# Mixer projections two column blocks at a time, with seven products for two or three of eight row pairs

## The chip, the cores and the metric

The kernel runs on one core of one Trainium2 chip. The metric is device time in microseconds (us) for the whole program: the median of three runs is 2322.91 us before the change (2322.89, 2323.82, 2322.91).

## The reference

A trunk of two layers over 256 tokens of width 2048, float32. Each layer is a token mixer beside a cross-attention to 256 memory tokens, one output projection, and a SwiGLU feed-forward net. Layer 0 has the HGRN2 mixer, layer 1 the GLA mixer. What matters here are the mixers' input projections:

```python
D_MODEL, SEQ = 2048, 256
MIX_WIDTH = 1536                      # the mixer's width
GLA_KEY_WIDTH = 768                   # GLA: 4 heads, key 192, value 384
def _hgrn2_mixer(hn, w_in, lb, onorm):
    proj = hn @ w_in                  # (256 x 2048) @ (2048 x 6656)
    q, f, i, g, xq = jnp.split(proj, [MIX_WIDTH, 2 * MIX_WIDTH, 3 * MIX_WIDTH, 4 * MIX_WIDTH], axis=-1)
    f = lb + (1.0 - lb) * jax.nn.sigmoid(f)
    ...
def _gla_mixer(hn, w_in, w_gk, b_gk, onorm):
    proj = hn @ w_in                  # q, k: 768 columns each; v, g: 1536 each
    ...
def reference(...):
    hn = _rmsnorm(h, norm_mix[layer])
    y, xq = _hgrn2_mixer(...) if layer % 2 == 0 else _gla_mixer(...)
    h = h + jnp.concatenate([y, xa], axis=-1) @ w_out[layer]
    gate, up = jnp.split(_rmsnorm(h, norm_ffn[layer]) @ w_gate_up[layer], 2, axis=-1)
    h = h + (jax.nn.silu(gate) * up) @ w_down[layer]
```

## The kernel before

**Tiles.** The 256 tokens are two tiles of 128, the 2048 rows of a weight matrix 16 blocks of 128, taken in eight row pairs. A weight tile comes from memory as float32 into `raw` (four buffers). `split` makes two tiles of it in TensorE's float32 format `F32R`: ScalarE casts it (L207, the high part), and VectorE subtracts that from the original (L208, the low part). Both lie in one of six `parts` buffers. Each product is three matmuls into one sum: high x high, high x low, low x high (L249 to L251). All sums live in eight PSUM banks. The left factors, transposed and split in the same way, are `Quad` tiles of four row blocks each (`hx` in layer 0, `hm` in layer 1; names end in `h` and `l`).

**Projections.** `project` takes one block of columns (512, or 384 for GLA's) through all 16 row blocks: per row pair 2 x 2 products, 12 matmuls for one block, and 24 for two blocks. The two sums are then read by ScalarE, which writes them to SBUF with the activation.

**The mixers.** `hgrn_group` runs three times, one group of four heads each: projections f, q, v, gate of 512 columns, one after the other. `gla_pair` runs twice, with two heads each: k and q of 384 columns, then gate and v of 384 columns for each of two heads. What lies between (the forget gates `F`, `K`, the decays `Th`, the masked scores `sl..` and `sd..`, reading the state, the gated norm, the transposes of the result) is cut into pieces, which `later` puts in a queue; `project` calls `step` after every second row block, and takes one piece each time.

**The feed-forward net.** `project_halves` already takes two column blocks at once, gate and up, and of its row pairs some ("S") with seven products in place of eight (24 matmuls become 21): a block has seven sums p1 to p7 in seven banks, and VectorE joins them at the block's end (L833). For that, an S pair takes differences of the four weight blocks on VectorE (L350 to L352) before they are split. Tiles are named by the pair's number: `parts185a` to `d`. The left factors come with forms for it (`s`, `u`, `z`, `d0` beside the four plain ones).

**What sets the order.** Each engine runs its instructions in the order of a list that a scheduler makes ahead of time, and so does the queue SP, which issues the DMAs. An instruction that waits holds up all that stand behind it on its engine.

Of the kernel before, what the change touches and what calls it, by code (L numbers as in the profile page):

```python
# [9 lines left out]
F32 = mybir.dt.float32  # L10
# [7 lines left out]
P = 128  # L18
# [17 lines left out]
def trunk_kernel(ctx: ExitStack, tc: tile.TileContext, x, mem, norm_mix, norm_ffn, norm_mem,  # L36
# [99 lines left out]
    class Quad:  # L136
# [5 lines left out]

        def put(self, k, n, ps, gain=None):
# [34 lines left out]
    def later(*pieces):  # L178
        pending.extend(pieces)
# [40 lines left out]
    def project(quads, order, w, c0, n, name, parts=None, prep=None, by_tile=None):  # L220
# [11 lines left out]
        for qis, ts in groups:  # L232
            for qi in qis:
# [5 lines left out]
                for k, (hi, lo) in enumerate(got[qi]):  # L239
# [4 lines left out]
                    for t in ts:  # L244
                        xh = quads[q].h[:, k, t * P:(t + 1) * P]
                        xl = quads[q].l[:, k, t * P:(t + 1) * P]
# [73 lines left out]

    def project_halves(forms, kinds, w, c0, c1, name):
# [15 lines left out]
        for p, kind in enumerate(kinds):  # L337
            i, raw = new_raw()

            for j, c in ((slice(0, 4, 3), c0), (slice(1, 3), c1)):  # L340
                nc.sync.dma_start(out=raw[:, j, :],
                                  in_=w[2 * p * P:(2 * p + 2) * P, c:c + 512].rearrange("(k p) c -> p k c", p=P))
            x = forms[p].get
            last = p == len(PAIRS) - 1
            if kind == "S":
                tt = nc.vector.tensor_tensor
                b00, = split(raw[:, 0:1, :], f"{i}a")
                b11, b10 = split(raw[:, 2:4, :], f"{i}b")

                tt(out=raw[:, 0:2, :], in0=raw[:, 0:4:2, :], in1=raw[:, 1:2, :].broadcast_to([P, 2, 512]), op=ALU.subtract)  # L350
                tt(out=raw[:, 2, :], in0=raw[:, 2, :], in1=raw[:, 0, :], op=ALU.add)  # L351
                tt(out=raw[:, 3, :], in0=raw[:, 3, :], in1=raw[:, 2, :], op=ALU.subtract)  # L352
                t5, t7 = split(raw[:, 0:2, :], f"{i}c")
                t6, t4 = split(raw[:, 2:4, :], f"{i}d")
                todo = {1: ("x00", b00), 2: ("x01", b10), 3: ("z", b11), 4: ("x11", t4), 5: ("s", t5), 6: ("u", t6),
                        7: ("d0", t7)}
# [19 lines left out]
    def h_quad(hq, q, gain, ss, name):  # L376

        for t in range(NT):
            square_sum(h[:, t, q * 512:(q + 1) * 512], ss[:, t, q:q + 1], f"{name}{q}{t}")

        def turn():
            hq[q] = make_quad(Quad("hq", f"{name}{q}"),
                              lambda k, t: h[:, t, (4 * q + k) * P:(4 * q + k + 1) * P],
                              lambda k: gain[:, 4 * q + k:4 * q + k + 1])

        later(turn)
# [48 lines left out]
    for l in range(2):  # L435
# [17 lines left out]
        if l == 0:  # L453
            load_params()
            hq, ss = {}, new_ss("ss_x")
            for q in range(NQ):
                h_quad(hq, q, g_mix[0], ss, "hx")
# [180 lines left out]
    def hgrn_group(w, g, hq, r, yq):  # L638
# [3 lines left out]
        def stage(c0, name, func):  # L642
            ps = project(hq, range(NQ), w, c0 + 512 * g, 512, f"h{name}{g}")
            tag, bufs = ("stg", 2) if name in "fq" else (name, 1)
            dst = work.tile([P, NT, 512], F32, tag=tag, name=f"{name}s{g}", bufs=bufs)
            for t in range(NT):
                nc.scalar.activation(out=dst[:, t, :], in_=ps[t], func=func, scale=r[:, t:t + 1])
            return dst
# [52 lines left out]
    def gla_pair(w, pr, dec, decay, hq, r, yq):  # L701
# [4 lines left out]
        def stage(c0, name):  # L706
            ps = project(hq, range(NQ), w, c0 + pr * 2 * DK, 2 * DK, f"g{name}{pr}")
# [41 lines left out]
        ks = stage(kw, "k")  # L749
        later(turn_k)  # L750
        qs = stage(0, "q")
# [206 lines left out]
```

## Time and profile before

| | |
|---|---|
| runs | 2322.89, 2323.82, 2322.91 us; median 2322.91 |
| profiled execution | 2322.1 us, of which the span is 2320.3 us |
| TensorE (PE) busy | 2297.6 us, 99% |
| VectorE (DVE) busy | 1887.7 us, 81% |
| ScalarE (ACT) busy | 1261.2 us, 54% |
| DMA | 435.51 MB, mean 188 GB/s |

A row of a timeline has the start in us from the span's start, the duration, the engine, the line of the program, and the operation with output, inputs and shape; in square brackets stands the idle time before it and what ended it. Instructions of an engine overlap in part: the next one starts before the last has ended, so that the cost of one in a row of them is the distance from start to start. A row of the table of stretches has the stretch, its length, the busy time of PE, of PE's weight loads, of DVE, of ACT and of POOL (each with the count of instructions), the granted TensorE clock, the share of DMA time and GB/s.

### The profile page before, as it was taken

To read this page: it belongs to the slowest core of one execution; us is meant where nothing else is said; L and a number is where in the kernel's file an instruction comes from. 1 tells how busy PE (TensorE), PEld (TensorE's weight loads), DVE (VectorE), ACT (ScalarE), POOL (GpSimd) and SP (SyncE) were. 2 spreads that over 40 slices of the span, in tenths; PEclk is the share of its full clock that TensorE was granted. 3 is DMA by queue.
4 is the path that set the end of the run, shared out by engine and by line. 5 is a ranking of instruction groups with operands and counts; after the bars stand their busy time and mean duration, and the time that the engine had idled before them with its cause. 6 is when DMAs were issued, how large, how long until landed. Compare 5 with 4: busy or idle time off the path is not lost.

```text
span 2320.3 us, 28901 instructions
## 1 busy us (share of the span) xinstructions
PE 2297.6 (99%) x11034; PEld 1934.7 (83%) x11034; DVE 1887.7 (81%) x2262; ACT 1261.2 (54%) x1643; POOL 22.2 (1%) x39
## 2 busy tenths in 40 slices
PE   9999999999999999999999999999999999999998
PEld 7888888888887888888889999988887888888886
DVE  5566565668999999999985665567999999999995
ACT  7543534455555555555555654455555555555563
POOL 0000000000000000000000000000000000000000
PEclk9999999999999999999999999999999999999999
DMA  8554545455556556566565445555555556656563
GB/s 316 192 172 162 164 150 176 145 182 176 186 188 212 200 188 205 189 209 208 183 226 167 150 150 167 161 199 164 178 203 198 201 187 210 202 189 210 200 217 127
DMA packets 229211, 435.51 MB, mean 188 GB/s; under 512 B 10028, under 2 KB 38992, under 8 KB 228816
## 3 DMA queue, kind: packets, MB, share of 16 engines
q1 hardware_dynamic: 227776, 429.40, 55.5%
q10 hardware_dynamic: 1296, 4.26, 0.5%
q8 instruction: 86, 1.41, 0.2%
q14 instruction: 53, 0.43, 0.1%
HBM read 430.48 MB, written 3.15 MB: 187 GB/s over the span
## 4 chain that ended last, share of the span: by engine, by line
PE 63%; DVE 25%; issue 6%; ACT 4%; DMA 0%; ACTq 0%; DVEq 0%; POOLq 0%; SPq 0%
PE f_p L334 5%; PE f_p L335 5%; PE f_p L333 4%; DVE raw L350 4%; DVE parts L208 4%; PE fd L250 3%; PE fd L249 3%; PE fd L251 3%; PE wo L251 3%; PE wo L249 3%; PE wo L250 3%; DVE raw L351 2%; DVE raw L352 2%; PE hgate L249 1%; PE gv L249 1%
## 5 line engine op out<-in xcount | busy, mean ns | idle before, releaser
L208 DVE TENSOR_TENSOR parts<-raw,parts 128x1024 fp32r<-128x1024 f32 (+3 forms) x490 | 557.7, 1147 | 289.1 <-ACT parts L207 288.2
L207 ACT CAST parts<-raw 128x1024 fp32r<-128x1024 f32 (+3 forms) x490 | 476.8, 991 | 424.6 <-PE wo L251 64.4
L350 DVE TENSOR_TENSOR raw<-raw 128x1024 f32<-128x1024 f32 x118 | 143.6, 1217 | 0.2
L351 DVE TENSOR_TENSOR raw<-raw 128x512 f32<-128x512 f32 x118 | 81.6, 692 | 3.9
L352 DVE TENSOR_TENSOR raw<-raw 128x512 f32<-128x512 f32 x118 | 81.6, 692 | 3.8
L414 DVE TENSOR_TENSOR h<-fd,h 128x512 f32<-128x512 f32 x94 | 61.9, 684 | 6.2 <-PE fd L251 6.1
L833 DVE TENSOR_TENSOR e<-f_p,e 128x512 f32<-128x512 f32 x66 | 44.9, 680 | 0.0
L835 ACT ACTIVATE s<-s,rf_r 128x512 f32<-128x512 f32 x44 | 31.8, 722 | 6.9 <-DVE s L833 6.9
L836 DVE SCALAR_TENSOR_TENSOR s<-e,rf_r,s 128x512 f32<-128x512 f32 x44 | 32.3, 742 | 0.0
L562 DVE COPY_PREDICATED sch<-mask,slh 96x512 f32<-96x512 uint8 (+3 forms) x15 | 10.8, 721 | 25.1 <-PE slh L578 25.1
L833 DVE TENSOR_TENSOR s<-f_p,e 128x512 f32<-128x512 f32 x44 | 29.5, 682 | 0.0
L578 PEld LDWEIGHTS slh<-Q,K 128*96 128x96 f32 (+3 forms) x240 | 25.4, 176 | 1.4
L249 PE MATMUL wo<-parts,y_3h 128*128 128x512 f32 x64 | 25.9, 405 | 0.0
L249 PE MATMUL wo<-parts,y_0h 128*128 128x512 f32 x64 | 25.7, 402 | 0.0
L250 PE MATMUL fd<-parts,s_3h 128*128 128x512 f32 x64 | 25.4, 396 | 0.0
L249 PE MATMUL fd<-parts,s_0h 128*128 128x512 f32 x64 | 25.3, 396 | 0.0
L249 PE MATMUL fd<-parts,s_2h 128*128 128x512 f32 x64 | 25.3, 396 | 0.0
L249 PE MATMUL fd<-parts,s_6h 128*128 128x512 f32 x64 | 25.3, 396 | 0.0
L249 PE MATMUL fd<-parts,s_4h 128*128 128x512 f32 x64 | 25.3, 396 | 0.0
L250 PE MATMUL fd<-parts,s_5h 128*128 128x512 f32 x64 | 25.3, 396 | 0.0
L249 PE MATMUL fd<-parts,s_8h 128*128 128x512 f32 x64 | 25.3, 396 | 0.0
L250 PE MATMUL fd<-parts,s_0h 128*128 128x512 f32 x64 | 25.3, 396 | 0.0
(5486 smaller groups left out, 7396.4 us busy)
## 6 DMA issues: line engine op xcount, KB each, us to landing
raw<-in_w_gate_up_dram SPq DMA_DIRECT2D x352, 512.0 KB, 4.0
raw<-in_w_down_dram SPq DMA_DIRECT2D x88, 1024.0 KB, 5.0
raw<-in_hgrn_w_in_dram SPq DMA_DIRECT2D x52, 1024.0 KB, 5.0
raw<-in_gla_w_in_dram SPq DMA_DIRECT2D x48, 768.0 KB, 4.3
raw<-in_w_out_dram SPq DMA_DIRECT2D x32, 1024.0 KB, 4.9
raw<-in_w_mem_kv_dram SPq DMA_DIRECT2D x15, 1024.0 KB, 8.2
raw<-in_gla_w_in_dram SPq DMA_DIRECT2D x8, 528.0 KB, 3.7
mtok<-in_mem_dram SPq DMA_DIRECT2D x4, 512.0 KB
```

The costliest lines, as they stand in the source:

```text
L207: nc.scalar.copy(out=both[:, 0, k:j, 0:m], in_=src[:, k:j, :])
L208: nc.vector.tensor_tensor(out=both[:, 1, k:j, 0:m], in0=src[:, k:j, :], in1=both[:, 0, k:j, 0:m].bitcast(F32), op=ALU.subtract)
L249: nc.tensor.matmul(acc, xh, hi[:, o:o + m], start=first, stop=False)
L250: nc.tensor.matmul(acc, xh, lo[:, o:o + m], start=False, stop=False)
L251: nc.tensor.matmul(acc, xl, hi[:, o:o + m], start=False, stop=last)
L333: nc.tensor.matmul(ps[b], xh, hi, start=first, stop=False)
L334: nc.tensor.matmul(ps[b], xh, lo, start=False, stop=False)
L335: nc.tensor.matmul(ps[b], xl, hi, start=False, stop=left[b] == 0)
L350: tt(out=raw[:, 0:2, :], in0=raw[:, 0:4:2, :], in1=raw[:, 1:2, :].broadcast_to([P, 2, 512]), op=ALU.subtract)
L351: tt(out=raw[:, 2, :], in0=raw[:, 2, :], in1=raw[:, 0, :], op=ALU.add)
L352: tt(out=raw[:, 3, :], in0=raw[:, 3, :], in1=raw[:, 2, :], op=ALU.subtract)
L833: nc.vector.tensor_tensor(out=out, in0=ps[p], in1=q, op=ALU.add)
```

## The change

`project_two` takes two column blocks at once in the mixers: f with q, and v with gate in HGRN; k with q, and gate with v in GLA. The first `n_seven` of the eight row pairs take seven products into seven banks (21 matmuls where two blocks of the plain way have 24). `n_seven` is 3, but 2 for v and gate of HGRN's third group and for the two gate-and-v stages of GLA's second pair. Then, in mid-stage, the seven sums are joined: ScalarE copies p1 to SBUF, and seven additions on VectorE leave the plain sums in banks 2, 4, 5 and 3. The remaining plain pairs accumulate onto these four banks. Pieces of the queue are taken in the plain pairs alone. A seven-pair goes through `seven`, which is the code of the net's S pair, moved. `h_quad` makes its left factors as `Pair` tiles, three of them with the four further forms, and the cross-attention's projection of layer 0 takes its quads in the order 2, 3, 0, 1. The stream of row pairs loads each pair with two DMAs of half the bytes (717 DMAs issued by SP, 621 before; the same bytes). There are 17 seven-pairs of 512 columns and 16 of 384; PE has 99 matmuls fewer (10,547 for 10,646), VectorE 279 more tensor-tensor operations (2212 for 1933), ScalarE 90 more copies (1225 for 1135). New line numbers: splits L210 and L211, differences L336 to L338, products L405 to L407, copy of p1 L418, additions L421, F L768, K L771.

```diff
+    def load_pair(raw, w, p, c0, c1, n):
+        for j, c in ((slice(0, 4, 3), c0), (slice(1, 3), c1)):
+            nc.sync.dma_start(out=raw[:, j, 0:n],
+                              in_=w[2 * p * P:(2 * p + 2) * P, c:c + n].rearrange("(k p) c -> p k c", p=P))
...
+    def seven(i, raw):
+        n = raw.shape[2]
+        tt = nc.vector.tensor_tensor
+        b00, = split(raw[:, 0:1, :], f"{i}a")
+        b11, b10 = split(raw[:, 2:4, :], f"{i}b")
+        tt(out=raw[:, 0:2, :], in0=raw[:, 0:4:2, :], in1=raw[:, 1:2, :].broadcast_to([P, 2, n]), op=ALU.subtract)
+        tt(out=raw[:, 2, :], in0=raw[:, 2, :], in1=raw[:, 0, :], op=ALU.add)
+        tt(out=raw[:, 3, :], in0=raw[:, 3, :], in1=raw[:, 2, :], op=ALU.subtract)
+        t5, t7 = split(raw[:, 0:2, :], f"{i}c")
+        t6, t4 = split(raw[:, 2:4, :], f"{i}d")
+        return {1: ("x00", b00), 2: ("x01", b10), 3: ("z", b11), 4: ("x11", t4), 5: ("s", t5), 6: ("u", t6), 7: ("d0", t7)}
...
+    class Pair:
...
+            g = work.tile([P, 8, P], F32, tag="stg", name=f"{self.name}g", bufs=2)
+            for k in range(2):
+                a = slice(2 * k, 2 * k + 2)
+                nc.scalar.activation(out=g[:, a, :], in_=v[:, a, :], func=AF.Copy, scale=gains[k])
+            tt = nc.vector.tensor_tensor
+            nc.vector.scalar_tensor_tensor(out=g[:, 4, :], in0=g[:, 1, :], scalar=-1.0, in1=g[:, 3, :],
+                                           op0=ALU.mult, op1=ALU.subtract)
+            tt(out=g[:, 5, :], in0=g[:, 0, :], in1=g[:, 1, :], op=ALU.subtract)
+            tt(out=g[:, 6, :], in0=g[:, 3, :], in1=g[:, 5, :], op=ALU.subtract)
+            tt(out=g[:, 7, :], in0=g[:, 2, :], in1=g[:, 6, :], op=ALU.subtract)
+            for part, j in ((self.main, 0), (self.more, 4)):
+                nc.scalar.copy(out=part[:, 0], in_=g[:, j:j + 4, :])
+                tt(out=part[:, 1], in0=g[:, j:j + 4, :], in1=part[:, 0].bitcast(F32), op=ALU.subtract)
...
+    def project_two(pairs, n_seven, w, c0, c1, n, name, e):
+        ps = {}
...
+        for p in range(n_seven):
+            i, raw = new_raw()
+            load_pair(raw, w, p, c0, c1, n)
+            todo = seven(i, raw[:, :, 0:n])
+            last = p == n_seven - 1
+            for b in (1, 2, 6, 7, 5, 4, 3) if last else (1, 3, 2, 5, 7, 6, 4):
+                product(b, pairs[p].get(todo[b][0]), todo[b][1], p == 0, last)
+        p_ = {b: t[:, 0:n] for b, t in ps.items()}
+        e0, e1 = e[:, 0, :], e[:, 1, :]
+        nc.scalar.copy(out=e0, in_=p_[1])
+        for out, a, b in ((p_[2], p_[2], e0), (e1, p_[6], e0), (e0, p_[7], e1), (e1, p_[5], e1),
+                          (p_[4], p_[4], e0), (p_[5], p_[5], e0), (p_[3], p_[3], e1)):
+            nc.vector.tensor_tensor(out=out, in0=a, in1=b, op=ALU.add)
+        for p in range(n_seven, len(PAIRS)):
+            i, raw = new_raw()
+            load_pair(raw, w, p, c0, c1, n)
+            b00, b01 = split(raw[:, 0:2, 0:n], f"{i}a")
+            b11, b10 = split(raw[:, 2:4, 0:n], f"{i}b")
+            for k, (left, right) in enumerate(((b00, b01), (b10, b11))):
+                step()
+                last = k == 1 and p == len(PAIRS) - 1
+                for b, t, right_factor in ((2, 0, left), (4, 1, left), (5, 1, right), (3, 0, right)):
+                    product(b, pairs[p].x(k, t), right_factor, False, last, True)
+        return [ps[2], ps[4]], [ps[3], ps[5]]
...
+    SEVEN = 3
...
-        fs = stage(MIX, "f", AF.Sigmoid)
-        later(turn_f)
-        qs = stage(0, "q", AF.Silu)
-        later(turn_q, None, *gated_scores(st, [[0], [1], [2], [3]], f"h{g}"))
-        v = stage(2 * MIX, "v", AF.Copy)
-        gate = stage(3 * MIX, "gate", AF.Silu)
+        fs, qs = stages(SEVEN, (MIX, "f", AF.Sigmoid), (0, "q", AF.Silu))
+        later(turn_f, turn_q, None, *gated_scores(st, [[0], [1], [2], [3]], f"h{g}"))
+        v, gate = stages(SEVEN - (g == 2), (2 * MIX, "v", AF.Copy), (3 * MIX, "gate", AF.Silu))
...
-        ps = project(hq, range(NQ), w, 4 * MIX, XA, "hx")
+        later(*first_turns)
+        ps = project(hq, (2, 3, 0, 1), w, 4 * MIX, XA, "hx")
...
+        psk, psq = project_two(hq["pairs"], SEVEN, w, kw + pr * 2 * DK, pr * 2 * DK, 2 * DK, f"gk{pr}", e)
...
+            both = project_two(hq["pairs"], SEVEN - pr, w, 2 * kw + MIX + (2 * pr + a) * DV, 2 * kw + (2 * pr + a) * DV, DV,
+                               f"gg{pr}{a}", e)
```

Where the change lets instructions fall, at two places. The first is VectorE in HGRN's second group, the stage that computes f and q, at the join of the seven sums. `parts38` is the third seven-pair of the stage, `parts39` the first plain pair, `hf1p2` to `hf1p7` are the stage's sums, `ef1` is the buffer of the join; `sch0` and `Q0` belong to the scores of the group before. After the change:

```order
L211 TENSOR_TENSOR parts38c_1957<-raw38_1945,parts38c_1957 128x1024
L670 COPY_PREDICATED sch0_1688<-mask_88,slh016_2001 112x32x16
L211 TENSOR_TENSOR parts38d_1960<-raw38_1945,parts38d_1960 128x1024
L211 TENSOR_TENSOR parts39a_1995<-raw39_1992,parts39a_1995 128x1024
L421 TENSOR_TENSOR ef1_1859<-hf1p6_1898,ef1_1859 128x512
L211 TENSOR_TENSOR parts39b_1998<-raw39_1992,parts39b_1998 128x1024
L421 TENSOR_TENSOR ef1_1859<-hf1p7_1894,ef1_1859 128x512
L682 TENSOR_TENSOR Q0_1636<-Q0_1636,Th0_1617 128x32x16
L421 TENSOR_TENSOR ef1_1859<-hf1p5_1890,ef1_1859 128x512
L421 TENSOR_TENSOR hf1p4_1902<-hf1p4_1902,ef1_1859 128x512
```

The last row writes the bank onto which the first plain pair's products for the second token tile go; before the change no such additions stood in a mixer's stage. PE at the same place, after the change:

```order
L405 MATMUL hf1p4_1902<-parts38d_1960,hx2x_932 128x512
L405 MATMUL hf1p2_1886<-parts39a_1995,hx3x_950 128x512
L406 MATMUL hf1p6_1898<-parts38d_1960,hx2m_933 128x512
L407 MATMUL hf1p6_1898<-parts38d_1960,hx2m_933 128x512
L406 MATMUL hf1p4_1902<-parts38d_1960,hx2x_932 128x512
L407 MATMUL hf1p4_1902<-parts38d_1960,hx2x_932 128x512
L406 MATMUL hf1p2_1886<-parts39a_1995,hx3x_950 128x512
L407 MATMUL hf1p2_1886<-parts39a_1995,hx3x_950 128x512
L405 MATMUL hf1p2_1886<-parts39b_1998,hx3x_950 128x512
L406 MATMUL hf1p2_1886<-parts39b_1998,hx3x_950 128x512
L407 MATMUL hf1p2_1886<-parts39b_1998,hx3x_950 128x512
L405 MATMUL hf1p2_1886<-parts40a_2052,hx4x_551 128x512
```

The next row on PE is the first product onto `hf1p4` that needs the join. Nine matmuls stand between the last one into p6 and it, and all of them go to p4's own sum or to p2, whose addition stands earlier.

The second place is VectorE in the same group, the stage that computes v and gate. Before the change, `F1` and `K1` (the forget gates of the second group, from the transposes `tf10` and `tf11` on PE) stood between the splits of plain rows, whose tiles are `parts42` and `parts43`:

```order
L208 TENSOR_TENSOR parts42_0_2091<-raw42_2089,parts42_0_2091 128x1024
L208 TENSOR_TENSOR parts42_2_2094<-raw42_2089,parts42_2_2094 128x1024
L657 TENSOR_SCALAR F1_2021<-tf10_2023,lbt_96 128x256 x2
L657 TENSOR_SCALAR F1_2021<-tf11_2030,lbt_96 128x256 x2
L208 TENSOR_TENSOR parts43_0_2123<-raw43_2121,parts43_0_2123 128x1024
L660 TENSOR_SCALAR K1_2022<-F1_2021 128x1024
```

After the change `parts45` and `parts46` are the second and third seven-pair of this stage, and `parts47` is the first plain one:

```order
L768 TENSOR_SCALAR F1_2412<-tf10_2414,lbt_96 128x256
L768 TENSOR_SCALAR F1_2412<-tf11_2421,lbt_96 128x256 x2
L211 TENSOR_TENSOR parts46d_2371<-raw46_2356,parts46d_2371 128x1024
L211 TENSOR_TENSOR parts47a_2406<-raw47_2403,parts47a_2406 128x1024
L421 TENSOR_TENSOR ev1_2270<-hv1p6_2309,ev1_2270 128x512
L211 TENSOR_TENSOR parts47b_2409<-raw47_2403,parts47b_2409 128x1024
L421 TENSOR_TENSOR ev1_2270<-hv1p7_2305,ev1_2270 128x512
L771 TENSOR_SCALAR K1_2413<-F1_2412 128x1024
L421 TENSOR_TENSOR ev1_2270<-hv1p5_2301,ev1_2270 128x512
L421 TENSOR_TENSOR hv1p4_2313<-hv1p4_2313,ev1_2270 128x512
```

`F1` and `K1` now stand among the seven-pairs' splits and inside the join. The first of the four rows of `F1`, which takes the first transposes of `tf10`, stands nine rows above these, ahead of `parts45d` and with that ahead of everything of the third seven-pair.

More of the change, by code (lines that the diff above doesn't have):

```diff
@@ L345, in project_halves @@
             if kind == "S":
[L346 to L356, printed above, removed]
+                todo = seven(i, raw)
                 for b in (1, 2, 6, 7, 5, 4, 3) if last else (1, 3, 2, 5, 7, 6, 4):
@@ L381, in turn @@
         def turn():
[L382 to L386, printed above, removed]
+            both = []
+            for p in (2 * q, 2 * q + 1):
+                both.append(Pair(f"{name}{p}", p < SEVEN))
+                ps = transposes([lambda t, c=(2 * p + k) * P: h[:, t, c:c + P] for k in range(2)], f"tp_{name}{p}")
+                both[-1].put(ps, [gain[:, 2 * p + k:2 * p + k + 1] for k in range(2)])
+            hq[q] = Pairs(*both)
+            hq.setdefault("pairs", {}).update({2 * q: both[0], 2 * q + 1: both[1]})
+        queue(turn)
     def h_forms(forms, n, gain, ss, name):
```

82 lines of the change are left out of this document (59 added, 23 removed).

## The prediction

> **What bounds the kernel now.** The page comes first: span, busy shares, DVE in 40 slices.
>
> ```profile
> span 2320.3 us, 28901 instructions
> PE 2297.6 (99%) x11034; PEld 1934.7 (83%) x11034; DVE 1887.7 (81%) x2262; ACT 1261.2 (54%) x1643; POOL 22.2 (1%) x39
> DVE  5566565668999999999985665567999999999995
> ```
>
> PE is busy all the time, so a matmul taken away is time won, as long as PE stays fed. The slices of DVE at 5 and 6 tenths are the mixers, those at 9 the feed-forward net. Closer in it is seen in the table of stretches: a block of the feed-forward net, one HGRN group, one stretch of GLA.
>
> ```profile
> 1045.20:1108.40 63.20, 62.97 (x279) 51.22 (x280) 62.48 (x71) 36.13 (x42) 0.00 (x0) 1.00 0.59 199
> 295.00:400.00 105.00, 105.00 (x555) 89.47 (x554) 62.57 (x81) 46.78 (x68) 2.92 (x3) 1.00 0.49 160
> 1310.00:1430.00 120.00, 120.00 (x741) 118.05 (x740) 71.06 (x107) 66.61 (x99) 3.28 (x7) 1.00 0.51 159
> ```
>
> In the net, where seven-pairs are already in use, DVE is as full as PE (62.48 of 63.20). The granted clock is full (1.00). In the mixers PE has no gap and DVE is idle four tenths of the time. By averages there is room: an HGRN group lasts from one group's scores to the next,
>
> ```profile
> 189.57 1.73 PE sdh L578 x16
> 294.54 1.73 PE sdh L578 x16
> 1321.21 1.73 PE sdg L578 x16
> 1442.15 1.73 PE sdg L578 x16
> ```
>
> 105.0 us, and a GLA pair 120.9 us. The question is whether the room lies where the new work comes.
>
> **What is saved.** The pitch of matmuls, start to start:
>
> ```profile
> 225.24 0.39 PE L251 MATMUL hgate<-parts,hx2l 128*128 128x512 f32 x1
> 229.34 0.39 PE L251 MATMUL hgate<-parts,hx2l 128*128 128x512 f32 x1
> 1386.10 0.33 PE L249 MATMUL gv<-parts,hm_1h 128*128 128x384 f32 x1
> 1390.78 0.33 PE L249 MATMUL gv<-parts,hm_2h 128*128 128x384 f32 x1
> ```
>
> 18 matmuls lie between the first two rows (0.2278 us each, 512 columns), 27 between the others (0.1733, 384 columns). Each seven-pair has three fewer: 17 x 3 x 0.2278 = 11.6 and 16 x 3 x 0.1733 = 8.3, together **19.9 us**.
>
> **What DVE has to do for it.** The net's seven-pair 185, and the plain pair 186 behind it:
>
> ```profile
> 1072.53 0.68 DVE L208 TENSOR_TENSOR parts185a<-raw,parts185a 128x512 fp32r<-128x512 f32 x1
> 1073.13 1.22 DVE L208 TENSOR_TENSOR parts185b<-raw,parts185b 128x1024 fp32r<-128x1024 f32 x1
> 1074.26 1.22 DVE L350 TENSOR_TENSOR raw<-raw 128x1024 f32<-128x1024 f32 x1
> 1075.52 0.69 DVE L351 TENSOR_TENSOR raw<-raw 128x512 f32<-128x512 f32 x1
> 1076.24 0.69 DVE L352 TENSOR_TENSOR raw<-raw 128x512 f32<-128x512 f32 x1
> 1076.85 1.22 DVE L208 TENSOR_TENSOR parts185c<-raw,parts185c 128x1024 fp32r<-128x1024 f32 x1
> 1078.13 1.23 DVE L208 TENSOR_TENSOR parts185d<-raw,parts185d 128x1024 fp32r<-128x1024 f32 x1
> 1079.27 1.22 DVE L208 TENSOR_TENSOR parts186a<-raw,parts186a 128x1024 fp32r<-128x1024 f32 x1
> 1081.54 0.68 DVE L208 TENSOR_TENSOR parts187a<-raw,parts187a 128x512 fp32r<-128x512 f32 x1
> ```
>
> A seven-pair takes DVE 6.74 us, a plain one 2.27. PE needs 21 x 0.2278 = 4.78 us for the first and 5.47 for the second. So in a run of seven-pairs DVE falls back 2 us with each, and gains 3 with each plain one. The net mixes the two kinds; here the three seven-pairs stand together at the stage's head, and at their end come seven additions whose results PE needs at once. In the net the next block writes other banks, so the additions there are off PE's path. How far ahead can DVE start? Six `parts` buffers: while PE runs the first seven-pair (four tiles), one tile of the second is ready, and one buffer still belongs to the pair before. The fifth tile's cast stands behind the evacuation of the stage before on ACT:
>
> ```profile
> 236.42 0.39 PE L251 MATMUL hgate<-parts,hx3l 128*128 128x512 f32 x1
> 236.85 1.37 ACT L647 ACTIVATE gates<-hgate,rx_r 128x512 f32<-128x512 f32 x2 [1.41 <-PE hgate L251]
> 238.11 1.04 ACT L207 CAST parts<-raw 128x1024 fp32r<-128x1024 f32 x1
> ```
>
> 0.43 us from the last matmul to ACT, 0.69 for a bank, 1.05 for the cast: DVE begins the second pair's tile b at 2.2 us from PE's start of the stage.
>
> The other prices: an addition from PSUM, a masked copy, a step of Q, the forget gates F and K, a 768-wide split, PE's scores and transposes.
>
> ```profile
> 1052.70 0.68 DVE L833 TENSOR_TENSOR e<-f_p,e 128x512 f32<-128x512 f32 x1
> 1053.30 0.68 DVE L833 TENSOR_TENSOR e<-f_p,s 128x512 f32<-128x512 f32 x1
> 325.06 0.72 DVE L562 COPY_PREDICATED sch<-mask,slh 112x512 f32<-112x512 uint8 x1 [1.94 <-PE slh L578]
> 325.67 0.68 DVE L574 TENSOR_TENSOR Q<-Q,Th 128x512 f32<-128x512 f32 x1
> 371.01 1.90 DVE L657 TENSOR_SCALAR F<-tf,lbt 128x256 f32<-128x256 f32 x4
> 373.96 0.68 DVE L660 TENSOR_SCALAR K<-F 128x1024 f32<-128x1024 f32 x1
> 1315.45 2.69 DVE L208 TENSOR_TENSOR parts<-raw,parts 128x768 fp32r<-128x768 f32 x3
> 229.57 1.49 PE L578 MATMUL slh<-Q,K 128*96 128x64 f32 x16
> 370.37 1.03 PE L160 MATMUL tf<-ident,fs 128*128 128x128 f32 x8
> ```
>
> **Stage f and q (the order's first place), from PE's first matmul.** DVE's rows from the second pair's tile b to the sum p4: eight splits of 1024 (8 x 1.14), one difference of 1024 (1.25), four of 512 (2 x 0.73 + 2 x 0.61), one split of 512 (0.60), five additions (p2, e1, e0, e1, p4; 5 x 0.60), the masked copy 0.62 and the step of Q 0.60. Sum 17.9, ready at 20.1. PE has 63 products of the seven-pairs and seven more into p2 ahead of the first that needs p4: 70 x 0.2278 = 15.9, with eight scores (0.86; two such groups take the row's 1.49 and some) 16.8. PE stands **3.3 us**; a bubble of about 1 us where ACT's cast waits for the differences would make it 4.4. I take 4. On PE all the plain pairs stand behind that product, and on DVE, behind the addition that waits for p6, the split of the next pair. Afterwards DVE gains 3 us with each of five plain pairs and has its whole lead back, so each stage pays anew. Three such stages: 12.
>
> **Stage v and gate (second place).** The first row of F needs transposes that PE reaches after 36 matmuls (8.2 us, with latency and the first rows about 9.0), and the third seven-pair stands behind it. From there to p4: F 4 x 0.46, six splits of 1024 (45d, 46b to 46d, 47a, 47b: 6.84), one of 512 (0.60), differences 1.25 + 0.73 + 0.61, five additions 3.0, K 0.60. Sum 15.5, ready at 24.5. PE arrives after 70 matmuls, sixteen transposes (2.06) and eight scores: 18.8. It stands **5.7 us**. With two seven-pairs (third group) I count 3.3. Three stages: 5.8 + 5.8 + 3.3 = 14.9.
>
> **GLA.** A 768-wide split is 0.87 to 0.90, and by halves between the 512 and 1024 rows an addition of 384 is about 0.48, differences 0.97 and 0.53 (estimates). For k and q of the second pair DVE needs 15.1 from a start at 1.8, ready at 16.9; PE comes after 73 x 0.1733 + 1.75 for scores = 14.4, and stands 2.5. In the first pair's two gate-and-v stages the steps of the decays and of Q among the splits make DVE's sum 15.7, ready at 17.5; PE, after 70 x 0.1733 and about 1 of transposes, stands 4.4 to 4.5 in each; with two seven-pairs 2 in each. 2.6 + 4.5 + 4.5 + 2.6 + 2 + 2 = 18.2.
>
> **Costed at nothing.** The 96 further DMA issues and the same bytes: the net loads in the same halves at 199 GB/s, and a seven-pair of 1 MB in 4.8 us, 218 GB/s, lasts for three pairs with four `raw` buffers as a cushion. Without it about 1 us a stage is lost, 12 in all; nothing can be gained. The further left forms are some 2 us on DVE (two rows of 512 at 0.60 and four small ones) for each of six tiles; the memory's projections (slices at 5) and the net's tail (8 and 5) cover them, and uncovered they would cost 12. ACT's copy of p1 (0.69, a bank) is early, since p1 is the first product of the last seven-pair.
>
> **Sum.** Stalls 12 + 14.9 + 18.2 = 45.1; saving 19.9; **net +25**. The profiled execution lasted 2322.1 (span 2320.3 and 1.8 around it): 2347.3; it lies 0.8 under the median, so 2348 for a median.
>
> The bounds of the stalls: the net shows what its last seven-pair does to PE,
>
> ```profile
> 1109.03 0.40 PE L335 MATMUL f_p<-parts191b,hf_7l 128*128 128x512 f32 x1
> 1109.66 0.50 PE L333 MATMUL f_p<-parts191d,hf_7h 128*128 128x512 f32 x1 [0.23 <-ACT parts191d L207]
> ```
>
> 0.63 in place of 0.23, so only 0.4 of waiting behind two seven-pairs in a row. If the mixers stalled no more than this, the stages would cost 5 us; if DVE were late everywhere by the bubble and the steps besides, 5.3 a stage, 63. I go near the walk, since it is made of durations alone; its own range is 2332 to 2366.
>
> **Rival 1: only the join costs (2326).** DVE keeps up through the seven-pairs. Still, from the last product into p6: 0.43 latency, addition 0.60, split 1.14, addition, step of Q, two additions 2.4, 0.1 to PE: 4.7, against nine matmuls on PE, 2.05. Over the twelve stages, by what stands in between, 1.3 to 2.65 each, 22.8 in sum: +3. For it: DVE is idle 40% of a group. Against: 6.74 against 4.78, three times running.
>
> **Rival 2: the waits are hidden, as in the net (2303 to 2318; faster).** If the wait at a join stays under 0.4 to 1.3 us, 5 to 15 of the 19.9 are lost. For it: PE keeps 99% in the net with DVE at 99%, while a group here would have DVE at 62.6 + 6 x 4.47 + 14 x 0.60 = 97.8 of 100.9. It decides if DVE enters a stage more than a tile ahead. Against: DVE takes its rows in order, and the split of the next pair's tile stands between the additions.
>
> **Rival 3: each join also costs clock (2368).** At the program's start PE comes out of idleness slowly:
>
> ```profile
> 5.33 1.91 PE L160 MATMUL tp_mem0h<-ident,mtok 128*128 128x128 f32 x8
> 7.46 1.22 PE L249 MATMUL mk<-parts,mem0h 128*128 128x512 f32 x2 [0.22 <-ACT parts L207]
> 8.90 0.51 PE L251 MATMUL mk<-parts,mem0l 128*128 128x512 f32 x1
> ```
>
> Eight transposes take 1.91 in place of 1.03, three matmuls of 512 columns 1.44 in place of 0.68: 1.6 us. At twelve joins that is 20: 2368. It decides if a single pause is as long as one that lowers the clock. Against: the clock is full in the stretches above, the pause at 1109.66 among them, and my stalls fall into two or three waits of about 2 us. [...]
>
> **How the numbers follow.** The walk 0.62, rival 1 0.14, rival 2 0.11, rival 3 0.13. What can be told from no change is 0.2%, 4.6 us: rival 2 is faster (0.11), half of rival 1 and a little more is the same (0.09), the rest slower (0.80). The range 2320 to 2370 leaves out rival 2 and the tails.
>
> **What will show it.** In the changed kernel's timeline of PE, waits released by DVE's additions (L421) ahead of the first product onto p4 in each stage, 2 us or more, and in the v-and-gate stages waits for `parts` of the third seven-pair besides; HGRN groups at 110 us and more (101 if all is hidden); DVE without a gap from each stage's head to the join, and idle after it; the clock at full. Waits at `raw` or a group period under 102 would make the prediction wrong, and so would waits of under 1 us at the joins.

## The result, and the profile after

The changed kernel takes 2359.14 us (median of four runs, 2358.65 to 2359.71) beside 2322.94 before: 1.0155 times as long, 95% interval 1.0137 to 1.0173. That is 36 us more, where 2348 and a range of 2320 to 2370 were forecast. The head of its page:

```profile
span 2357.7 us, 29278 instructions
PE 2307.0 (98%) x10935; PEld 1918.3 (81%) x10935; DVE 2053.2 (87%) x2535; ACT 1313.1 (56%) x1733; POOL 22.9 (1%) x39
DVE  5588788768999999999986877866999999999995
```

DVE's slices of 5 and 6 tenths in the mixers are now 7 and 8, and PE, with 99 matmuls fewer, is no longer at 99%. Where the time went, from the starts of the first matmuls of the stages in PE's timeline (us):

| stretch | before | after | difference |
|---|---|---|---|
| start to HGRN's first group | 126.31 | 127.35 | +1.0 |
| HGRN groups and output projection | 414.55 | 429.42 | +14.9 |
| feed-forward net of layer 0 | 703.41 | 703.51 | +0.1 |
| GLA's cross-attention projection | 23.92 | 23.92 | 0.0 |
| GLA pairs and output projection | 341.80 | 363.74 | +21.9 |
| net of layer 1, to the last matmul | 700.58 | 700.84 | +0.3 |

The saving of 11.6 us in HGRN and 8.3 in GLA lies inside these numbers, so PE lost 26.5 us in HGRN's stretch and 30.2 in GLA's. The nets are as long as before to 0.3 us. The second HGRN group, in the table of stretches (columns as in the table before: PE 104.73 us busy, DVE 94.08):

```profile
237.37:347.33 109.96, 104.73 (x536) 85.35 (x534) 94.08 (x126) 56.43 (x82) 2.92 (x3) 1.00 0.46 153
```

It lasts 110.0 us; 105.0 less the 4.1 of matmuls saved would be 100.9. PE's longest waits in the mixers of the changed kernel, by what ended them (total, times, longest; three more of 0.8 us for splits on DVE are left out):

```profile
PE gg01p L405 <- ACT ggate L874: 2.5, 1, 2.5
PE gg01p L405 <- ACT gv L874: 1.8, 1, 1.8
PE hf1p L405 <- DVE hf1p L421: 1.4, 1, 1.4
PE hf2p L405 <- DVE hf2p L421: 1.4, 1, 1.4
PE hv2p L405 <- DVE hv2p L421: 1.3, 1, 1.3
PE gg00p L405 <- ACT gsq L819: 1.2, 1, 1.2
PE gg00p L405 <- ACT parts233b L210: 1.2, 1, 1.2
PE gg00p L405 <- DVE gg00p L421: 0.9, 1, 0.9
PE hf1p L406 <- DVE parts39b L211: 0.8, 1, 0.8
PE hv1p L406 <- DVE parts47b L211: 0.8, 1, 0.8
```

Two kinds stand there: waits for DVE at the join (L421) and at the splits around it, which the prediction had, and waits of GLA's stages for ACT's evacuations (L874 and L819, ACT reading the finished sums out of their banks), which it had not. (L210 is ACT's cast, the first half of a split.) The join of the second group's stage f and q, on DVE and then on PE (there with rows left out between):

```profile
252.92 1.23 DVE L211 TENSOR_TENSOR parts39a<-raw,parts39a 128x1024 fp32r<-128x1024 f32 x1
254.06 0.69 DVE L421 TENSOR_TENSOR ef<-hf1p,ef 128x512 f32<-128x512 f32 x1
254.66 1.23 DVE L211 TENSOR_TENSOR parts39b<-raw,parts39b 128x1024 fp32r<-128x1024 f32 x1
255.79 0.70 DVE L421 TENSOR_TENSOR ef<-hf1p,ef 128x512 f32<-128x512 f32 x1
256.39 0.70 DVE L682 TENSOR_TENSOR Q<-Q,Th 128x512 f32<-128x512 f32 x1
256.99 0.70 DVE L421 TENSOR_TENSOR ef<-hf1p,ef 128x512 f32<-128x512 f32 x1
257.59 1.90 DVE L421 TENSOR_TENSOR hf1p<-hf1p,ef 128x512 f32<-128x512 f32 x3
```

```profile
237.36 0.39 PE L405 MATMUL hf1p<-parts36a,hx0x 128*128 128x512 f32 x1
248.92 0.71 PE L686 MATMUL slh<-Q,K 128*112 128x64 f32 x6
249.43 0.71 PE L405 MATMUL hf1p<-parts38c,hx2m 128*128 128x512 f32 x2
249.98 1.10 PE L686 MATMUL slh<-Q,K 128*112 128x64 f32 x10
255.94 0.50 PE L406 MATMUL hf1p<-parts39b,hx3x 128*128 128x512 f32 x1 [0.78 <-DVE parts39b L211]
258.35 0.50 PE L405 MATMUL hf1p<-parts39a,hx3x 128*128 128x512 f32 x1 [1.44 <-DVE hf1p L421]
```

DVE has no gap here, and PE reaches the first plain product onto p4 20.99 us after the stage's first matmul. Its own work up to there is 17.4: 70 x 0.2278 = 15.95 for the products, and 1.4 for eight scores, which are sixteen rows in the trace (0.51 us for the first six, start to start, and about 0.9 for the other ten). Between the last product into p6 (253.41) and this one stand eight matmuls, two onto p4's own sum and six onto p2; the text ahead of the prediction counts nine.

### The profile page after: what moved, and what is told of

It is laid out like the page before. It is cut to its first block, busy times and chain, and to the rows that moved or that the text cites. A ratio compares the mean times of both kernels' runs of the same rounds, so it can differ in the third digit from the quotient of the medians.

```text
span 2357.7 us, 29278 instructions
## 1 busy us (share of the span) xinstructions
PE 2307.0 (98%) x10935; PEld 1918.3 (81%) x10935; DVE 2053.2 (87%) x2535; ACT 1313.1 (56%) x1733; POOL 22.9 (1%) x39
## 4 chain that ended last, share of the span: by engine, by line
PE 53%; DVE 33%; issue 8%; ACT 6%; DMA 0%; ACTq 0%; DVEq 0%; POOLq 0%; POOL 0%; SPq 0%
DVE raw L336 5%; DVE parts L211 4%; PE f_p L447 4%; PE f_p L448 4%; PE f_p L446 3%; PE fd L252 3%; PE fd L253 3%; PE fd L251 3%; DVE raw L337 3%; DVE raw L338 3%; PE wo L251 2%; PE wo L253 2%; PE wo L252 2%; DVE e L945 1%; PE slh L686 1%
## 5 line engine op out<-in xcount | busy, mean ns | idle before, releaser
L211 DVE TENSOR_TENSOR parts<-raw,parts 128x1024 fp32r<-128x1024 f32 (+2 forms) x298 | 349.6, 1188 | 118.2 <-ACT parts L210 117.9
L210 ACT CAST parts<-raw 128x1024 fp32r<-128x1024 f32 (+2 forms) x298 | 295.9, 1021 | 178.5 <-PE wo L253 66.5
L336 DVE TENSOR_TENSOR raw<-raw 128x1024 f32<-128x1024 f32 (+1 forms) x151 | 180.1, 1193 | 0.8
L338 DVE TENSOR_TENSOR raw<-raw 128x512 f32<-128x512 f32 (+1 forms) x151 | 102.2, 677 | 4.3
L337 DVE TENSOR_TENSOR raw<-raw 128x512 f32<-128x512 f32 (+1 forms) x151 | 102.2, 677 | 4.3
L252 PE MATMUL fd<-parts,s_7h 128*128 128x512 f32 x64 | 25.3, 396 | 0.0
L252 PE MATMUL fd<-parts,s_1h 128*128 128x512 f32 x64 | 25.3, 396 | 0.0
```

What stands on the lines that cost most here:

```text
L210: nc.scalar.copy(out=both[:, 0, k:j, 0:m], in_=src[:, k:j, :])
L211: nc.vector.tensor_tensor(out=both[:, 1, k:j, 0:m], in0=src[:, k:j, :], in1=both[:, 0, k:j, 0:m].bitcast(F32), op=ALU.subtract)
L252: nc.tensor.matmul(acc, xh, lo[:, o:o + m], start=False, stop=False)
```

## The experiments

All times are medians, the ratios against runs of the kernel before on the same chip. The two right columns are the same stretches as above, from each run's own trace; those of before less the matmuls saved, with 17 and 16 seven-pairs, would be 402.95 and 333.5.

| version | us | ratio (95%) | HGRN + wo | GLA + wo |
|---|---|---|---|---|
| before | 2323 | 1 | 414.55 | 341.80 |
| after | 2359.1 | 1.0155 (1.0137 to 1.0173) | 429.42 | 363.74 |
| no seven-pair | 2327.2 | 1.0017 (1.0007 to 1.0026) | 416.60 | 343.85 |
| one in each stage | 2322.2 | 0.9995 (0.9986 to 1.0004) | 414.77 | 341.34 |
| two, decays earlier | 2337.0 | 1.0060 (1.0045 to 1.0075) | 422.70 | 346.62 |
| three in HGRN alone | 2339.7 | 1.0074 (1.0059 to 1.0089) | 429.40 | 343.88 |
| after, decays earlier | 2345.5 | 1.0098 (1.0081 to 1.0115) | 429.48 | 349.43 |
| the same, 7 split buffers, 3 raw | 2329.9 | 1.0028 (1.0019 to 1.0038) | 421.53 | 346.01 |
| after without the join | 2334.4 | 1.0048 (1.0033 to 1.0063) | 413.74 | 356.33 |
| after without the differences | 2319.3 | 0.9985 (0.9976 to 0.9994) | 405.90 | 349.99 |
| seven-pairs last | 2348.7 | 1.0110 (1.0095 to 1.0125) | 421.59 | 359.82 |
| seven-pairs last, decays earlier | 2347.1 | 1.0106 (1.0089 to 1.0122) | 421.26 | 359.27 |
| after, decays earlier, differences on GpSimd | 2408.4 | 1.0368 (1.0354 to 1.0382) | 468.45 | 376.06 |

**Is it the seven-pairs at all?** All pairs plain:

```diff
-    SEVEN = 3
+    SEVEN = 0
-        v, gate = stages(SEVEN - (g == 2), ...
+        v, gate = stages(SEVEN, ...
-            both = project_two(hq["pairs"], SEVEN - pr, ...
+            both = project_two(hq["pairs"], SEVEN, ...
+        if n_seven:                       # the join only then; the first plain pair starts the banks
```

> No pair takes seven products; two column blocks still go at a time, the pairs are loaded in halves and the queue's pieces fall as in the changed kernel's code. Theory (the loss lies in the seven-pairs and their join): PE's work is that of the kernel before, so 2323, within 2319 to 2328. Rival (the rearrangement itself costs: the evacuation of four banks at once, pieces in other places, the decays beside the evacuations on ACT): 2335 or more, with waits of PE for ACT at the heads of GLA's stages.

2327.2: the theory's range holds. Two blocks at a time, halves of loads and moved pieces cost 3.9 us with nothing saved. In the profiled execution HGRN and GLA are 2.05 longer each, and the start 1.3. Its trace shows PE waiting 1.3 us in three goes for the evacuation of f ahead of F's transposes, and 1.6 in two goes for that of v; what makes up the rest was not followed.

**How many seven-pairs does DVE's lead carry?** One in each stage (as above, with `SEVEN = 1`), and two (`SEVEN = 2`, with the decays moved as in the experiment on GLA's waits, below):

> One seven-pair in each stage: 6 x 3 x 0.2278 + 6 x 3 x 0.1733 = 7.2 us of matmuls saved. Theory (a join costs its chain even where DVE has its whole lead, 1.3 to 2.65 us a stage): 2327 - 7.2 + 22.8 = 2343, or somewhat less, 2335 to 2345. Rival (the join costs only because DVE comes to it late, after three seven-pairs): 2318 to 2324.

> Two seven-pairs in each stage, the second pair's decays three pieces earlier as in the 2345.5 us version with three: 12 x 2 x 3 matmuls fewer, 14.4 us. Theory (six buffers of lead cover one seven-pair, each further one puts DVE 2 us later): from one pair (2322.2) to two 12 x (2.0 - 0.6) = +17 at most, less what lead is left: 2330 to 2339. Rival (DVE's lead covers two, only the third is late): 2314 to 2321, faster than before.

With one, 2322.2 (no change): the join hardly costs when DVE comes to it on time, and the theory that it costs its chain in any case fell. With two, 2337.0, as the theory had it. Counted in HGRN's stretch, with 4.1 us of saving for each seven-pair in its six stages, PE's loss is 2.05 us with none, 4.3 with one, 16.4 with two and 26.5 with three (two in the last stage). The second pair costs 12 us over six stages, **2.0 a stage**, and the third 10.1 over five, 2.0 again; that is the lag of 6.74 - 4.78. The first is carried by the lead.

**What do DVE's two new burdens cost, each by itself?** The join left out, then the differences (both leave out work that the result needs, and PE's matmuls stay):

```diff
-        nc.scalar.copy(out=e0, in_=p_[1])
-        for out, a, b in ((p_[2], p_[2], e0), (e1, p_[6], e0), (e0, p_[7], e1), (e1, p_[5], e1),
-                          (p_[4], p_[4], e0), (p_[5], p_[5], e0), (p_[3], p_[3], e1)):
-            nc.vector.tensor_tensor(out=out, in0=a, in1=b, op=ALU.add)
```

> The join is left out (the copy of p1 and the seven additions): plain pairs go straight onto banks 2, 4, 5 and 3, and p1, p6 and p7 are never used, so that the output is another. Theory (DVE is late through seven-pairs and join together): without five additions ahead of p4 and the chain behind p6, DVE is at most about 1 us late in a stage; 2303 + 12 x 0.5 to 1, and some 8 for GLA's waits for ACT: 2315 to 2323. Rival (DVE is late through the differences and splits alone, the join lies in their shadow): 2340 to 2355. Rival (the join is everything): 2303 plus 8 for ACT, 2311.

```diff
-        tt(out=raw[:, 0:2, :], in0=raw[:, 0:4:2, :], in1=raw[:, 1:2, :].broadcast_to([P, 2, n]), op=ALU.subtract)
-        tt(out=raw[:, 2, :], in0=raw[:, 2, :], in1=raw[:, 0, :], op=ALU.add)
-        tt(out=raw[:, 3, :], in0=raw[:, 3, :], in1=raw[:, 2, :], op=ALU.subtract)
```

> In the mixers' seven-pairs the three differences of the weight blocks are left out (a wrong product, the same matmuls and splits): DVE spends 0.60 + 3 x 1.14 = 4.0 us on such a pair in place of 6.74, less than PE's 4.78. Theory: only the chain behind p6 remains, 1.3 to 2.65 us a stage, 22.8 in sum, of which 19.9 is won back, and some 8 for ACT's part in GLA: 2326 to 2336. Rival (the differences are everything, the chain is hidden once DVE keeps up): 2303 to 2313. Rival (the join is everything): 2355 to 2359, no change.

2334.4 and 2319.3; neither lies in the theory's range, nor in a rival's. In HGRN, where PE waits for no evacuation by ACT, leaving out the join takes 15.7 us off and leaving out the differences 23.5: together 39, more than the 26.5 that are lost. So the two do not add: they stand in one queue, and what one of them delays, the other need not delay again. Without the join 8.7 us over the 402.95 + 2.05 of the plain version remain, and PE still waits 5.5 us in ten goes for casts; without the differences HGRN lies 0.9 us over it, join and all. The reason stands in the order of the instructions: with DVE on time, 22 matmuls and eight scores stand on PE between the last product into p6 and the first plain one onto p4, where the changed kernel had eight matmuls. The short distance seems itself a sign of DVE's lateness: PE had been given other products to do while the third pair's tile d was on its way.

**GLA's waits for ACT.** What stood between the evacuations, in ACT's timeline at the end of the first pair's first gate-and-v stage, and PE's first waits in the next:

```profile
1376.09 1.06 ACT L918 ACTIVATE ab<-ab 128x1024 f32<-128x1024 f32 x1
1377.16 1.28 ACT L874 ACT_TABLE_LOAD   x1
1378.46 0.58 ACT L874 ACTIVATE ggate<-gg00p,rm_r 128x384 f32<-128x384 f32 x1
1379.06 1.28 ACT L919 ACT_TABLE_LOAD   x1
1380.36 1.06 ACT L919 ACTIVATE ab<-ab 128x1024 f32<-128x1024 f32 x1
1381.43 1.28 ACT L874 ACT_TABLE_LOAD   x1
1382.73 0.58 ACT L874 ACTIVATE ggate<-gg00p,rm_r 128x384 f32<-128x384 f32 x1
1383.33 1.28 ACT L921 ACT_TABLE_LOAD   x1
1384.62 1.06 ACT L921 ACTIVATE GF<-GF 128x1024 f32<-128x1024 f32 x1
1385.58 1.03 ACT L874 ACTIVATE gv<-gg00p,rm_r 128x384 f32<-128x384 f32 x2
```

```profile
1383.36 0.45 PE L405 MATMUL gg01p<-parts240d,hm_0m 128*128 128x384 f32 x1 [2.52 <-ACT ggate L874]
1386.20 0.69 PE L405 MATMUL gg01p<-parts240d,hm_0x 128*128 128x384 f32 x1 [1.83 <-ACT gv L874]
```

ACT alternates between the evacuations of four banks (L874) and the decays of the second pair (L918 to L921), and loads an activation table at each change, 1.28 us four times over. The next stage needs seven banks at once, where the kernel before needed two. The decays were put three pieces earlier:

```diff
-            scores[5:5] = [lambda: decay(1), None]
+            scores[2:2] = [lambda: decay(1), None]
```

> The decays of GLA's second pair go three pieces earlier in the queue, so that their three activations with table loads no longer stand between the evacuations of the first pair's first gate-and-v stage on ACT. Theory (the waits of 2.5 and 1.8 us for banks in the next stage and the half clock after them come from these): 8 to 10 us are won, 2349 to 2352. Rival (DVE would be late there anyway): 2356 to 2359.

2345.5: 13.7 us less, more than the 8 to 10 expected, and all in GLA (14.3); HGRN is the same to 0.1. The waits of 2.5 and 1.8 are gone from the list. PE's waits of 0.15 us and more in GLA's stretch fall from 14.0 to 6.1 us in sum, and the half clock there from 10.24 to 3.41 us, which is 3.4 us of work: 11.3 of the 14.3. The rest was not followed.

**HGRN by itself.** GLA's pairs plain (`n_seven` of both its calls 0):

> Seven-pairs in HGRN alone, all of GLA's pairs plain. Theory (HGRN's stalls and GLA's are apart, by the traces +14.9 us for HGRN with its output projection, +22 for GLA): 2323 + 14.9 + up to 3 for taking GLA's blocks two at a time: 2337 to 2341. Rival (the price is shared, by loading or by the left forms' cost before the layers): 2345 or more.

2339.7, as expected: HGRN costs the same 429.40 whatever GLA does, so the two layers' prices add.

**Is DVE's lead set by the six buffers?**

```diff
-        return i, wts.tile([P, 4, 512], F32, tag="raw", name=f"raw{i}", bufs=4)
+        return i, wts.tile([P, 4, 512], F32, tag="raw", name=f"raw{i}", bufs=3)
-        both = wts.tile([P, 2, 2, 512], F32R, tag="parts", name=f"parts{name}", bufs=6)
+        both = wts.tile([P, 2, 2, 512], F32R, tag="parts", name=f"parts{name}", bufs=7)
```

(The decays earlier, and the other tiles of the tag `parts` with seven buffers too.)

> The changed kernel with the decays earlier (2345.5), seven buffers for the split tiles in place of six and, for the room, three raw buffers in place of four. Theory (DVE's lead at a stage's head is set by the six buffers): in the mixers DVE comes one tile, 1.1 us, earlier to each join: the two layers' mixers take 8 to 13 us less, read from the trace of the mixers alone, 2333 to 2338 in all if the net does not feel the three raw buffers. Rival (the lead is set by ACT's evacuation and casts or by the loads): the mixers take the same, within 3 us, or more.

2329.9, 15.6 us less than with six. HGRN's stretch is 7.95 shorter, 1.3 for each of six stages, about the one tile of 1.14 us that was expected; GLA's 3.4, so that the mixers' 11.4 lie in the expected 8 to 13. The nets gain 1.6 and 1.5 us besides, with a `raw` buffer less, and with that the whole lies under the 2333 to 2338. It remains slower than the kernel before.

**Join at the stage's end.** Plain pairs first, the seven-pairs last, the product for the right half's second token tile in an eighth bank:

```diff
-        for p in range(n_seven):          # seven-pairs, join, then
-        for p in range(n_seven, len(PAIRS)):   # plain pairs onto banks 2, 4, 5, 3
+        for p in range(n_seven, len(PAIRS)):   # plain pairs into banks 2, 4, 8, 3
+        for p in range(n_seven):          # seven-pairs: 2, 4, 3 go on; 1, 5, 6, 7 begin
+        for out, a, b in ((e1, p_[6], e0), (p_[2], p_[2], e0), (e0, p_[7], e1), (e1, p_[5], e1), (p_[4], p_[4], e0),
+                          (p_[3], p_[3], e1), (e1, p_[7], e1), (p_[8], p_[8], e1)):
```

> The plain pairs go first, the seven-pairs last, with the plain product of the right half for the second token tile in a bank of its own, so that the join comes at the end of a stage (eight additions) and the next stage starts on the banks of p1, p6 and p7, which come free first. Theory (the loss is that the additions lie on PE's path): DVE enters the seven-pairs with all six buffers full and nothing waits for the join but the evacuation; 2303 plus the 4 us that two blocks at a time cost, plus up to 1 us a stage: 2307 to 2319, faster than both. Rival (DVE's 2 us of lag with each seven-pair stops PE wherever the pairs stand, or the next stage waits for banks): 2330 to 2350.

> As the version with the seven-pairs last, and the decays of GLA's second pair three pieces earlier in the queue. With the pieces taken ahead of the seven-pairs the decays stand clear of the evacuations already, so within 2 us of that version. If ACT's table loads still hold up banks there: 3 to 10 us less.

2348.7 and 2347.1: the theory that the loss is only that the additions lie on PE's path fell too. HGRN gained 7.8 us on the changed kernel, GLA 3.9, and new waits came in place of the old:

```profile
PE gpo L740 <- ACT gv L874: 4.6, 1, 4.6
PE tf L163 <- DVE y_1l L155: 2.1, 2, 1.7
PE gk0p L405 <- ACT parts230d L210: 1.8, 1, 1.8
```

Readouts and transposes now wait for evacuations that follow a join, and DVE's late splits are at the stage's end in place of its middle. The decays had no part in it here, as expected.

**The differences on the idle engine.**

```diff
-            todo = seven(i, raw[:, :, 0:n])
+            todo = seven(i, raw[:, :, 0:n], nc.gpsimd)     # the engine of the three differences
```

> The changed kernel with the second pair's decays three pieces earlier (2345.5 by itself), and the three differences of the mixers' seven-pairs on GpSimd, which is idle, in place of VectorE. Theory (DVE's time for the differences makes it late, and with that the join): DVE spends 4.0 us on a seven-pair and PE 4.78, so the time goes to what leaving the differences out gave, less the decays' part: 2319.3 - 13.7 = 2306 to 2315, if GpSimd does 2048 elements in about 4 us (its fill of 1024 took 0.96, its cast of 512 took 0.61). Rival (GpSimd is slower than PE's 4.78 us for a pair, or holds up DVE beside it): 2325 to 2360, with waits of PE for the tiles c and d.

> The version with the seven-pairs last and the decays earlier (2347.1), and the differences on GpSimd. Theory (there too DVE is too full at the stage's end): 2310 to 2325. Rival (the cost there is the evacuation of four banks and the join at the stage's end): 2335 to 2347.

2408.4, and 2414.1 with the seven-pairs last (1.0392, 1.0378 to 1.0406). The groups of GpSimd's instructions of 512 columns in the first version (count, total, mean ns):

```profile
L336 POOL TENSOR_TENSOR raw<-raw 128x1024 f32<-128x1024 f32 x17 | 47.0, 2764 | 263.2 <-DVE parts20a L211 72.3 <-DVE parts36a L211 31.2 <-DVE parts28a L211 31.1
L337 POOL TENSOR_TENSOR raw<-raw 128x512 f32<-128x512 f32 x17 | 30.3, 1785 | 25.3 <-DVE parts29b L211 4.3 <-DVE parts61b L211 4.0 <-DVE parts45b L211 4.0
L338 POOL TENSOR_TENSOR raw<-raw 128x512 f32<-128x512 f32 x17 | 26.6, 1566 | 1.3
```

2.76 + 1.79 + 1.57 = 6.1 us for a pair, over PE's 4.78, so the rival's reason held: PE waits up to 5.8 us at a time for the tile d. Both times lie well over the rivals' ranges, which ended at 2360 and 2347.

A stage that mixes seven-pairs with plain ones, as the net does, was not tried.

## Why the prediction was right, and where it was not

The direction, the range and, for HGRN, the size were right; the sizes inside HGRN's sum are right in part by chance.

**Stage f and q.** The sum p4 was to be ready at 20.1 us, or 21.1 with the bubble; it was there at 20.8 (257.59 plus a pitch of 0.60, from 237.36), and the bubble is in the trace: DVE waits 1.20 us for ACT's cast of `parts37d` (244.10). PE's own work was put at 16.8 and is 17.4, because the walk took eight scores at 0.86 and they cost 1.4. PE's loss up to there is 20.99 - 17.4 = 3.6, where 4 was taken.

**Stage v and gate** stood as walked: p4 was expected at 24.5, and the three additions that begin with it start at 314.90, so at 315.5, 24.0 after the stage's first matmul at 291.46. PE came to it at 24.8. Its own work by the trace's pitches is 19.1, not 18.8 (eight scores 1.7 in place of 0.86, sixteen transposes 1.45 in place of 2.06), and its loss 5.7, as forecast. The wait took another place, since by then PE stood at the scores, which wait for K:

```profile
313.70 0.68 DVE L771 TENSOR_SCALAR K<-F 128x1024 f32<-128x1024 f32 x1
314.90 1.89 DVE L421 TENSOR_TENSOR hv1p<-hv1p,ev 128x512 f32<-128x512 f32 x3
314.44 2.00 PE L686 MATMUL sdh<-Q,K 128*128 128x64 f32 x16 [0.23 <-DVE K L771]
316.25 0.48 PE L405 MATMUL hv1p<-parts47a,hx3x 128*128 128x512 f32 x1
```

In the third group, with two seven-pairs, the loss up to p4 is 3.5, where 3.3 was forecast.

HGRN in sum: 12 + 14.9 = 26.9 of stalls forecast, 26.5 measured. The 26.5 hold 1.7 of half clock that the walk left out, and the version without seven-pairs loses 2.05 too, partly by waits (1.3 us for the evacuation of f) that the changed kernel does not show. So the agreement to 0.4 is closer than the walk deserves.

**The signs** held in part. An HGRN group takes 110.0 us, as forecast, and no wait is for `raw`. But the additions (L421) end only six of PE's waits, of 0.15 to 1.44 us, where 2 us or more were forecast in each of twelve stages; in nine of the twelve there is none or one of under 1 us, which the prediction had named as a sign against itself. The lateness was there, in smaller pieces: in HGRN PE waits 5.0 us for DVE's splits, 4.2 for the additions and 3.7 for ACT's casts. DVE was not without a gap either: besides the 1.20, it waits 4.14 us for ACT's cast of `parts45b` in stage v and gate (295.69). And the clock fell to 0.50 at two places (417.80 and 1383.78).

**GLA was the term that was mis-sized**: 18.2 forecast, 30.2 measured. The step that failed is "GLA", which counted DVE alone. The trace of before had the decays on ACT and four evacuations, and the order of the changed kernel showed the one between the other; neither was walked. Moving the decays gives 14.3 of it back. What remains, 15.9, is near the 18.2 by chance: it holds 1.7 of half clock and a wait of 1.2 for ACT's evacuation of q (L819), which the walk had not, so that at most 13 are left for DVE's part.

**Costed at nothing**: the loads are right, since no wait of PE in a mixer was ended by a transfer. The start is 1.0 us longer (126.31 before, 127.35 after; 126.56 to 127.65 in the versions). The latest, 127.65, is that of the version without seven-pairs, which makes no further left forms, so it need not be these; what it is stays open.

**Rival 1** (the join costs its chain even when DVE is on time) is refuted: without the differences HGRN's loss is 3 us, 2 of which the plain version has too, and with one seven-pair in each stage nothing is lost in all. (Its nine matmuls are eight, 1.82 us in place of 2.05.) **Rival 2** (all hidden) holds for one seven-pair only; its condition, a tile more of lead, is worth what the seventh buffer showed. **Rival 3** (clock) came true at two places, one of them a join, and not at twelve, below. The pause at 1109.66, which lies behind the stretches that the prediction shows, left the clock at 1.00 too (1108 to 1112 in the kernel before).

The sum gave 2347.3 for a profiled execution, and that of the changed kernel took 2359.5. The difference of 12.2 is 12.0 from GLA, 1.0 from the start and 0.4 from the nets, less 0.4 in HGRN and 0.9 behind the last matmul.

## What to carry to other kernels

A stage that PE bounds has room on another engine only within that engine's lead, and the buffers between the two set it: here six carry one seven-pair that takes DVE 2 us longer than PE, each further one costs those 2 us, however idle DVE is later in the stage, and a seventh buffer gave 1.3 us a stage back, about the time of one tile. Price such a change by walking one stage in the order of the instructions, for every engine that PE waits for, ACT's evacuations with their table loads among them, since a stage that takes more banks also waits for more of them (2.52 and 1.83 us here). Two burdens on one late engine do not add up: of the 26.5 us lost here, taking out the one gave 15.7 back and taking out the other 23.5.

## What the runs showed of the hardware

**Half clock after short pauses.** After the wait of 1.30 us in HGRN's last stage matmuls of 512 columns go at a pitch of 0.43 us. The row, and the granted clock (the third number from the end) behind it and in GLA after the waits of 2.52 and 1.83:

```profile
417.59 0.63 PE L405 MATMUL hv2p<-parts62a,hx2x 128*128 128x512 f32 x1 [1.30 <-DVE hv2p L421]
417.60:421.10 3.50, 3.50 (x9) 2.72 (x10) 3.50 (x6) 0.24 (x1) 0.00 (x0) 0.53 0.65 242
1386.00:1392.00 6.00, 5.80 (x24) 5.80 (x25) 2.39 (x3) 2.58 (x5) 0.00 (x0) 0.50 0.00 0
1380.00:1400.00 20.00, 15.24 (x74) 13.59 (x73) 10.75 (x16) 11.70 (x16) 0.00 (x0) 0.74 0.11 35
```

The first costs eight matmuls 0.2 us each and a ninth 0.1, 1.7 in all; the second up to (1 - 0.74) x 20 = 5.2, which is part of why moving the decays gave more than the waits. Yet pauses of 1.44 us at 258.35 and 368.32 left the clock at full, so the length of one pause does not decide. In the version with three in HGRN alone it is the other way round: the same pause, at 367.69, is followed by half clock from 368.52 on, and the one of 1.29 in the last stage (418.54) is not.

What the traces show is a grid. Within one run the falls begin whole multiples of 3.413 us apart: 417.80 and 1383.78 in the changed kernel, 283 of them, and so do all thirteen falls in the mixers of the version with the differences on GpSimd (139.45 to 1573.04, 420 of them). The stretches of this grid ahead of the fall at 417.80 and around the pause at 368.32, both of the changed kernel, and the one ahead of 368.52 in the version with three in HGRN alone:

```profile
414.39:417.80 3.41, 1.78 (x9) 1.05 (x8) 3.41 (x6) 3.41 (x7) 0.00 (x0) 1.00 1.01 360
366.60:370.01 3.41, 1.98 (x9) 1.42 (x8) 3.41 (x7) 0.33 (x1) 0.00 (x0) 1.00 1.03 371
365.11:368.52 3.41, 1.79 (x7) 1.17 (x8) 3.41 (x7) 1.19 (x2) 0.00 (x0) 1.00 1.06 368
```

PE is busy for 0.52, 0.58 and 0.52 of them, and the clock falls behind the first and the third. In the changed kernel's HGRN the stretch of 0.52 is the only one followed by half clock, and no other has a share under 0.58. In the 7 us up to the end of the pause at 417.59 PE stands 1.97 us in sum; in the version with two seven-pairs in each stage it stands 1.03 to 2.01 us in the 7 us up to the end of each of five pauses in HGRN, and the clock is at 1.00 in the 5 us behind each. So where a pause lies on the grid matters, and how much PE works beside it. The border is not sharp: in GLA of the version without the differences a fall at 1310.82 came behind a stretch in which PE was busy for 0.61 or more, while behind the 0.58 above there was none.

**GpSimd beside DVE.** With the differences on GpSimd, some of DVE's instructions that run beside them take longer: in that version's timeline

```profile
241.24 3.31 POOL L336 TENSOR_TENSOR raw<-raw 128x1024 f32<-128x1024 f32 x1 [31.18 <-DVE parts36a L211]
243.23 1.88 DVE L682 TENSOR_TENSOR Q<-Q,Th 128x512 f32<-128x512 f32 x1
246.71 2.28 DVE L211 TENSOR_TENSOR parts36c<-raw,parts36c 128x1024 fp32r<-128x1024 f32 x1
```

the step of Q takes 1.88 us in place of 0.70, and a split of 1024 takes 2.28 in place of 1.23. Others do not: the split of `parts36b`, which begins at 241.09, just ahead of GpSimd's row, takes 1.21, and an addition of the join, from PSUM, takes 0.70 beside GpSimd (205.28). So DVE's time over GpSimd's is not free time; which instructions pay was not followed further.
